# Block loads of a triangular inverse moved from the ScalarE to the SyncE queue, and a quarter of the weights' low parts moved to GpSimd

## The chip, the cores and the metric

The kernel runs on one core of one Trainium2 chip. The metric is the device time of one execution in microseconds, as the median of several runs. The engines are TensorE (PE; its weight loads are shown as PEld), VectorE (DVE), ScalarE (ACT), GpSimd (POOL) and SyncE (SP). DMAs are issued here from the queues of SyncE and ScalarE. An engine carries out its instructions in the order of its queue, so an instruction that waits holds up those behind it on the same engine.

## What is computed

Two layers of a decoder trunk on 256 tokens of width 2048, in float32. Cut to what matters:

```python
for l in range(DEPTH):                       # 2
    hn = rms_norm(h, norm_w[l])
    proj = hn @ w_in[l]                      # 2048 x 8208
    dn_qkv, dn_z, dn_b, dn_a, hg_q, hg_f, hg_i, hg_z = jnp.split(proj, split_points, axis=-1)
    y_a = deltanet_branch(...)               # per chunk: (A + I)^-1 applied, A strictly lower triangular
    y_b = hgrn2_branch(...)
    h = h + jnp.concatenate([y_a, y_b], axis=-1) @ w_out[l]       # 2048 x 2048
    gate = jax.nn.sigmoid(h @ w_ple_gate[l])                      # 2048 x 2048
    h = h + (p[l] @ w_ple_up[l]) * gate                           # 256 x 2048
return rms_norm(h, final_norm_w)
```

Each branch has eight heads of 128, which the kernel handles in four groups of two heads (g = 0 to 3).

## The kernel before

**Weight units.** All weights are packed in the order of use and cut into 392 units (`make_plan`), numbered n. A unit is 128 x 1024 numbers in most cases: two k-tiles of a chunk of 512 columns, or four k-tiles of a narrower chunk (272 or 256 columns). In each layer the input projection has 17 chunks (`in_order`) and 128 units: n = 0 to 127 in the first layer, n = 196 to 323 in the second. Units of chunks 0 and 1 alternate at the start of a layer. Chunk 16, the last, has the last eight units of the stage.

A matmul in full float32 is replaced by three in a faster format: a weight is split into a high part (`whi`, line L400, a copy on ScalarE with rounding) and a low part (`wlo`, L402, raw minus high, on VectorE), and the products are high by high, high by low and low by high. So each unit goes through a DMA from HBM into a raw buffer (`load`, L378, issued by SyncE), the split (`prep`), and 12 matmuls of 512 columns (`products`, L336). Raw, high and low buffers are three each. `ahead(n)` loads up to four units ahead of unit n and splits two units ahead. A load has to wait until the low part of the unit three before it has been made, since both parts are read from the raw buffer. A split waits until TensorE is done with the unit three before.

**Order.** TensorE's instructions keep the order of the program. Beside the units runs the work of the two branches ("mixers"), as generators that yield a number of steps to wait: `tick()` is called once behind each unit, and a generator goes on when its count has run out. The tables `DELAY` and `DELAY_AT` hold the counts, by kind, group and step (`d0q` is DeltaNet, group 0, step q). The other engines' queues are laid out at build time by readiness and program order.

**The inverse.** `Inverse.run` is started when all four DeltaNet groups have delivered their matrices (`given`). It inverts the 16 x 16 diagonal blocks on VectorE (X, L653 and L656), writes them to a scratch in DRAM (`d2`, L658, ScalarE's queue), waits w steps, and reads them back as eight blocks into the tile `Tt` (L662, eight DMAs of 16 KB on ScalarE's queue, all at once). It waits T steps and doubles the block size three times: VectorE transposes (L671), products `pp` and `px` on TensorE, and copies back into `Tt` (L690 with a mask, L712, L740), with waits t16, p16 and so on between them. When it is done, `ready` is set, and each DeltaNet group takes its part (`pz`, in `dv`). In the first layer the waits t16 and p16 are 5 and 1 steps, in the second 2 and 2.

**Work of GpSimd before.** It makes the decay's arguments (`ug`, L769), gate products (`sz`, L590), triangular masks of `QK` (L866), and clears `Tt` (L643).

**Evictions.** Behind each chunk of the input projection, ScalarE copies the sums out of PSUM (`evict`, L597, to a tile named like `hg01fqet`), and the bank is then free for a later chunk.

Of the kernel before, what the change touches and what calls it, by code (L numbers as in the profile page):

```python
# [8 lines left out]
F32 = mybir.dt.float32  # L9
# [3 lines left out]
ALU = mybir.AluOpType  # L13
PSUM = bass.MemoryType.PSUM

DEPTH, D, T, KT = 2, 2048, 256, 16
# [15 lines left out]
def chunk_cols(chunk):  # L32

    return [(START[k], 16) if k == "ba" else (START[k] + 256 * g, 256) for k, g in chunk]
# [2 lines left out]

DELAY = {
    "d": {'c': 1, 'D': 4, 'k': 6, 'q': 7, 'ssq': 1, 'v': 5, 'z0': 1, 'S': 1, 'w': 1, 'z1': 1, 'o': 1, 'y': 3, 'yp': 1},
    "i": {'F': 4, 'F2': 1, 'F3': 1, 'F4': 1, 'w': 2, 'T': 6, 't16': 3, 'p16': 2, 't32': 3, 'p32': 2, 't64': 3, 'p64': 2},  # L40
    "b": {'o': 1, 'g': 4},
    "h": {'c': 1, 'f': 1, 'x2': 1, 'x4': 1, 'x8': 1, 'a': 2, 'x16': 1, 'x32': 1, 'x64': 1, 'u16': 2, 'u64': 1, 'o': 2, 'y': 2, 'yp': 1, 'q': 0},
}

DELAY_AT = {
    "b1g": 5,
    "d0q": 6, "d0y": 2, "d0z1": 2,
    "d2D": 3, "d2k": 4, "d2o": 2, "d2q": 9, "d2y": 2,
    "d3D": 5, "d3ssq": 3,
    "h0o": 4, "h0u16": 1, "h0u64": 3, "h0y": 3, "h0yp": 2,  # L50
    "h1c": 3, "h1o": 1, "h1q": 1, "h1x32": 3, "h1x8": 3, "h1yp": 4,
    "h2c": 2, "h2f": 2, "h2q": 2,
# [10 lines left out]
def in_order():  # L63

    kq = lambda g: (("dk", g), ("dq", g))
    vz = lambda g: (("dv", g), ("dz", g))
    fq = lambda g: (("hf", g), ("hq", g))
    iz = lambda g: (("hi", g), ("hz", g))
    return [(("dz", 0), ("ba", 0)), kq(0), kq(1), kq(2), kq(3), fq(0), iz(0), fq(1), iz(1), fq(2), (("dv", 0),), vz(1),
            iz(2), vz(2), fq(3), vz(3), iz(3)]  # L70
# [96 lines left out]
def trunk(ctx: ExitStack, tc: tile.TileContext, head, xT, x, pT, W, par, fw, cst, msk, eye, out):  # L167
    nc = tc.nc
# [12 lines left out]
    V, S, G = nc.vector, nc.scalar, nc.gpsimd  # L181
# [100 lines left out]
    d2 = dr.tile([256 * 128], F32, name="d2")  # L282
# [20 lines left out]
    def bc1(ap, n):  # L303
        return ap.unsqueeze(1).to_broadcast([ap.shape[0], n, ap.shape[1]])
# [82 lines left out]
    def prep(n):  # L387
        s = steps[n]
        f = s["n"] * len(s["kts"])
        raw = raws.pop(n)  # L390
        if n >= len(steps) - 2:

            ready[n] = [split(raw[:, 512 * j:512 * j + 512], j, None, f"w{n}") for j in range(2)]
            return
        hi = ws.tile([128, 1088], F32R, tag="whi", name=f"whi{n}")
        lo = ws.tile([128, 1088], F32R, tag="wlo", name=f"wlo{n}")
        w = f // 4 if n < 2 else f
        parts = [slice(j, j + w) for j in range(0, f, w)]
        for sl in parts:
            S.activation(hi[:, sl], raw[:, sl], AF.Copy)  # L400
        for sl in parts:
            V.tensor_tensor(lo[:, sl], raw[:, sl], hi[:, sl].bitcast(F32), ALU.subtract)  # L402
        ready[n] = [(hi[:, j * s["n"]:(j + 1) * s["n"]], lo[:, j * s["n"]:(j + 1) * s["n"]]) for j in range(len(s["kts"]))]

    def ahead(n):
        while state["loaded"] < min(len(steps), n + 1 + LOAD) or state["prepped"] < min(len(steps), n + 1 + LOOK):
            if state["loaded"] < min(len(steps), n + 1 + LOAD, state["prepped"] + WRAW):
                load(state["loaded"])
                state["loaded"] += 1
            else:  # L410
                prep(state["prepped"])
                state["prepped"] += 1
# [23 lines left out]
    def run_step(psums, act):  # L436

        n = state["next"]
        s = steps[n]
        ahead(n)  # L440
        if not n:
            for j in range(4):
                for i in (0, 2, 1):
                    for m in range(2):
                        products(n, m, psums, act, js=(j,), parts=(i,))
                if j == 1:
                    warm(1)
        for m in range(2):
            if n:
                products(n, m, psums, act)  # L450
        del ready[n]
        state["next"] = n + 1
        if s["what"] != "up":
            tick()
        return s
# [25 lines left out]
    def split(src, kp, scales, name):  # L481

        hi = ap_.tile([128, 2 * T], F32R, tag="ahi", name=f"{name}hi{kp}")
        lo = ap_.tile([128, 2 * T], F32R, tag="alo", name=f"{name}lo{kp}")
        if scales is None:
            S.activation(hi, src, AF.Copy)
            V.tensor_tensor(lo, src, hi.bitcast(F32), ALU.subtract)
            return hi, lo
        w = 2 * T // len(scales)
        for j, sc in enumerate(scales):  # L490
            S.activation(hi[:, w * j:w * j + w], src[:, w * j:w * j + w], AF.Copy, scale=sc)
        for j, sc in enumerate(scales):
            sl = slice(w * j, w * j + w)
            V.scalar_tensor_tensor(lo[:, sl], src[:, sl], sc, hi[:, sl].bitcast(F32), ALU.mult, ALU.subtract)
        return hi, lo
# [68 lines left out]
    def mix(tag, n, bufs, name):  # L564
        return mp.tile([128, n], F32, tag=tag, name=name, bufs=bufs)

    def v4(ap):
        return ap.rearrange("p (a b) -> p a b", b=128)
# [43 lines left out]
    class Inverse:  # L612


        NT = 4 * NG
# [21 lines left out]
        def run(self):  # L637
            n, Bt, NT = self.n, self.Bt, self.NT


            Tt = self.Tt = v4(mix("Tt", 128 * NT, 1, n + "Tt"))
# [3 lines left out]
            F, X = fx[:, 0], fx[:, 1]  # L645
# [3 lines left out]
            for c in range(1, 16):  # L649
# [3 lines left out]
                i = V.tensor_tensor(pr_[:, :c, :c], X[:, :c, :c], bc1(F[:, :c, c], c), ALU.mult)  # L653
# [5 lines left out]
            yield self.wait("w")  # L659
            for j in range(8):  # L660
                b = slice(16 * j, 16 * j + 16)
                nc.scalar.dma_start(out=Tt[b, :, b], in_=d2.rearrange("(i b a c) -> b a i c", i=NT, b=8, a=16)[j])  # L662
            yield self.wait("T")


# [4 lines left out]
            for b in blocks:  # L670
                i = V.transpose(Tn[b:b + 32], Tt[b:b + 32, :, b:b + 32])  # L671
# [52 lines left out]
            for i in range(NT):  # L724
                for b in (64, 96):
                    c = 64 * (i % 8)
# [7 lines left out]
            for i in range(NT):  # L734
                for b in (0, 32):
                    c = 64 * (i % 8)
# [520 lines left out]
    for l in range(DEPTH):  # L1257
# [25 lines left out]
        for c, k4 in order:  # L1283
# [5 lines left out]
            w = 2 if sum(n for _, n in chunk_cols(ch)) > 272 else 4  # L1289
            for q in range(0, 4, w):  # L1290
# [19 lines left out]
                s = run_step(ps[c], act)  # L1310
# [28 lines left out]
        for c, k4 in order:  # L1339
# [15 lines left out]
            if end and k4[3] == KT - 9:  # L1355

                n = state["next"]
# [46 lines left out]
```

## Time and profile before

| | |
|---|---|
| median of 3 runs | 1256.43 us (1256.11 to 1256.9) |
| profiled execution | 1256.09 us, its span 1254.4 us |
| mean granted TensorE clock | 0.995 |
| PE busy | 1232.5 us (98% of the span) |
| DVE busy | 878.6 us (70%) |
| ACT busy | 779.7 us (62%) |
| POOL busy | 68.5 us (5%) |
| DMA | 218.71 MB, 174 GB/s on average |

Busy time is the time in which an engine had an instruction at work. Matmuls overlap one another, so that a busy PE isn't necessarily at its peak. In rows of the profile, `out<-in` gives the tiles that an instruction writes and reads, `x8` a count, and a bracket the idle time of the engine before the instruction with what ended it. `ACTq` and `SPq` are DMA issues on an engine's queue. Times in the timeline are us from the start of the span, then the duration.

### The profile page before, as it was taken

How to read it: one execution, taken by the hardware profiler on the slowest of the kernel's cores; microseconds unless marked ns; L12 is line 12 of the kernel's file. 1: busy time of each engine (PE TensorE's matmuls, PEld its weight loads, DVE VectorE, ACT ScalarE, POOL GpSimd, SP SyncE). 2: the span in 40 equal slices, each digit the busy share in tenths (PEclk: the TensorE clock that was granted, in tenths of full speed). 3: DMA queues.
4: the chain of work that ended last, by engine and by line, in shares of the span. 5: the costliest groups of instructions: out<-in, count | busy, mean ns of one | idle time of the engine just before them, and what ended most of it. 6: DMA issues, size and time to landing. Idle time of an engine off the chain costs nothing.

```text
span 1254.4 us, 21620 instructions
## 1 busy us (share of the span) xinstructions
PE 1232.5 (98%) x8385; PEld 1034.9 (83%) x8385; DVE 878.6 (70%) x1520; ACT 779.7 (62%) x1397; POOL 68.5 (5%) x64
## 2 busy tenths in 40 slices
PE   9999998999999999999999999989999999999996
PEld 7888887798888888888888888877988888888886
DVE  7777795968668656547667887877776695565566
ACT  7676765676657744447656777566776676444464
POOL 0310000000000100000003100000000000000010
PEclk9999999999999999999999999999999999999998
DMA  8555555545564455555655655645454546555563
GB/s 276 184 178 172 172 173 146 167 134 171 168 218 152 169 178 182 185 192 181 190 182 167 181 159 173 193 120 160 132 164 154 179 145 198 196 183 182 184 202 135
DMA packets 73719, 218.71 MB, mean 174 GB/s; under 512 B 15504, under 2 KB 20752, under 8 KB 73616
## 3 DMA queue, kind: packets, MB, share of 16 engines
q1 hardware_dynamic: 59040, 211.52, 52.6%
q10 hardware_dynamic: 14576, 5.80, 1.7%
q8 instruction: 66, 1.08, 0.3%
q14 instruction: 37, 0.30, 0.1%
HBM read 212.84 MB, written 4.46 MB: 173 GB/s over the span
## 4 chain that ended last, share of the span: by engine, by line
PE 83%; DVE 10%; ACT 2%; issue 2%; DMA 2%; ACTq 0%; SPq 0%; DVEq 0%
PE out L336 14%; PE gate L336 14%; PE in0dk L336 7%; PE in0dv L336 6%; PE in1dk L336 6%; PE in1hf L336 5%; PE in0hf L336 5%; PE in1dv L336 5%; PE in0hi L336 4%; PE in1hi L336 4%; DVE wlo L402 3%; PE up L336 2%; PE in1dz L336 1%; ACT whi L400 1%; PE in0dz L336 1%
## 5 line engine op out<-in xcount | busy, mean ns | idle before, releaser
L402 DVE TENSOR_TENSOR wlo<-raw,whi 128x1024 fp32r<-128x1024 f32 (+1 forms) x392 | 482.1, 1232 | 288.4 <-ACT whi L400 287.6
L400 ACT ACTIVATE whi<-raw 128x1024 fp32r<-128x1024 f32 (+1 forms) x392 | 411.6, 1052 | 333.5 <-PE out L336 89.6
L336 PE MATMUL in1hi<-whi,n1hi 128*128 128x512 f32 x128 | 52.3, 408 | 2.3 <-ACT hg11fqet L597 2.3
L336 PE MATMUL in1hf<-wlo,n1hi 128*128 128x512 f32 x128 | 50.0, 391 | 2.7 <-issue 1.4
L336 PE MATMUL in1dk<-whi,n1hi 128*128 128x512 f32 x128 | 51.2, 400 | 0.0
L336 PE MATMUL in1hf<-whi,n1hi 128*128 128x512 f32 x128 | 51.2, 400 | 0.0
L336 PE MATMUL in1dk<-wlo,n1hi 128*128 128x512 f32 x128 | 50.0, 391 | 0.7 <-DVE wlo L402 0.7
L336 PE MATMUL in1hi<-whi,n1lo 128*128 128x512 f32 x128 | 50.4, 393 | 0.0
L336 PE MATMUL in1hi<-wlo,n1hi 128*128 128x512 f32 x128 | 50.2, 392 | 0.0
L336 PE MATMUL gate<-whi,g0hi 128*128 128x512 f32 x128 | 50.1, 392 | 0.0
L336 PE MATMUL in1dk<-whi,n1lo 128*128 128x512 f32 x128 | 50.0, 391 | 0.0
L336 PE MATMUL in1hf<-whi,n1lo 128*128 128x512 f32 x128 | 49.9, 390 | 0.0
L336 PE MATMUL gate<-whi,g0lo 128*128 128x512 f32 x128 | 49.8, 389 | 0.0
L336 PE MATMUL gate<-wlo,g0hi 128*128 128x512 f32 x128 | 49.8, 389 | 0.0
L336 PE MATMUL in1dv<-whi,n1hi 128*128 128x512 f32 (+1 forms) x128 | 48.2, 377 | 0.0
L336 PE MATMUL in1dv<-whi,n1lo 128*128 128x512 f32 (+1 forms) x128 | 46.6, 364 | 0.0
L336 PE MATMUL in1dv<-wlo,n1hi 128*128 128x512 f32 (+1 forms) x128 | 46.5, 363 | 0.0
L336 PE MATMUL gate<-whi,g1hi 128*128 128x512 f32 (+1 forms) x120 | 45.5, 379 | 0.0
L336 PE MATMUL gate<-wlo,g1hi 128*128 128x512 f32 (+1 forms) x120 | 45.4, 379 | 0.0
L336 PE MATMUL gate<-whi,g1lo 128*128 128x512 f32 (+1 forms) x120 | 45.4, 378 | 0.0
L336 PE MATMUL in0hi<-whi,n0hi 128*128 128x512 f32 x96 | 38.6, 402 | 0.0
L336 PE MATMUL in0hf<-whi,n0hi 128*128 128x512 f32 x96 | 38.4, 400 | 0.0
(1495 smaller groups left out, 3174.8 us busy)
## 6 DMA issues: line engine op xcount, KB each, us to landing
raw<-W SPq DMA_DIRECT2D x384, 512.0 KB, 3.5
raw<-W SPq DMA_DIRECT2D x7, 544.0 KB, 4.2
h<-x SPq DMA_DIRECT2D x4, 512.0 KB, 4.6
xt<-xT SPq DMA_DIRECT2D x3, 512.0 KB, 6.6
out_dram<-h SPq DMA_DIRECT2D x6, 256.0 KB, 2.2
di0d<-di0Bt ACTq DMA_DIRECT2D x4, 256.0 KB, 2.8
di1d<-di1Bt ACTq DMA_DIRECT2D x4, 256.0 KB, 2.3
fw<-fw ACTq DMA_DIRECT2D x2, 512.0 KB, 4.2
```

What stands on the lines that cost most here:

```text
L336: return tc.keep_in_program_order(nc.tensor.matmul(*a, **k))
L400: S.activation(hi[:, sl], raw[:, sl], AF.Copy)
L402: V.tensor_tensor(lo[:, sl], raw[:, sl], hi[:, sl].bitcast(F32), ALU.subtract)
```

## The change

Three things are changed. First, the eight block loads of `Tt` are issued by SyncE instead of ScalarE, with a wait of one step (`b`) behind each, and the wait `T` behind them is 2 steps instead of 6. Second, for every fourth unit of the input projection (n % 4 == 3), from unit 32 on and except in the first and the last chunk, GpSimd subtracts the low part instead of VectorE; nothing else of the unit is changed. Third, four delays of the DeltaNet groups are changed: group 0's `D` is 3 instead of 4 and its `q` 7 (the table's value) instead of 6, group 3's `q` is 5 instead of 7 and its `ssq` 5 instead of 3.

```diff
 DELAY = {
...
-    "i": {'F': 4, 'F2': 1, 'F3': 1, 'F4': 1, 'w': 2, 'T': 6, 't16': 3, 'p16': 2, 't32': 3, 'p32': 2, 't64': 3, 'p64': 2},
+    "i": {'F': 4, 'F2': 1, 'F3': 1, 'F4': 1, 'w': 2, 'b': 1, 'T': 2, 't16': 3, 'p16': 2, 't32': 3, 'p32': 2, 't64': 3, 'p64': 2},
...
 DELAY_AT = {
-    "d0q": 6, "d0y": 2, "d0z1": 2,
+    "d0D": 3, "d0y": 2, "d0z1": 2,
...
-    "d3D": 5, "d3ssq": 3,
+    "d3D": 5, "d3q": 5, "d3ssq": 5,
...
         for sl in parts:
             S.activation(hi[:, sl], raw[:, sl], AF.Copy)
+
+        on = G if s["what"] == "in" and n >= 32 and n % 4 == 3 and s["c"] not in (0, len(in_order()) - 1) else V
         for sl in parts:
-            V.tensor_tensor(lo[:, sl], raw[:, sl], hi[:, sl].bitcast(F32), ALU.subtract)
+            on.tensor_tensor(lo[:, sl], raw[:, sl], hi[:, sl].bitcast(F32), ALU.subtract)
...
             yield self.wait("w")
             for j in range(8):
                 b = slice(16 * j, 16 * j + 16)
-                nc.scalar.dma_start(out=Tt[b, :, b], in_=d2.rearrange("(i b a c) -> b a i c", i=NT, b=8, a=16)[j])
+                nc.sync.dma_start(out=Tt[b, :, b], in_=d2.rearrange("(i b a c) -> b a i c", i=NT, b=8, a=16)[j])
+                yield self.wait("b")
             yield self.wait("T")
```

## The prediction, before the result was known

> **What bounds the kernel now.** I read the page first, then the busy time by stretches, the waits, the chain of waits, and the timeline around the places where TensorE stands still.
>
> ```profile
> PE 1232.5 (98%) x8385; PEld 1034.9 (83%) x8385; DVE 878.6 (70%) x1520; ACT 779.7 (62%) x1397; POOL 68.5 (5%) x64
> L402 DVE TENSOR_TENSOR wlo<-raw,whi 128x1024 fp32r<-128x1024 f32 (+1 forms) x392 | 482.1, 1232 | 288.4 <-ACT whi L400 287.6
> ```
>
> TensorE is busy for 98% of the span, so 21.9 us is all the idle time there is. VectorE is busy for 70%, and more than half of that is one operation, the low part of a weight unit (1.23 us, 392 times). An average hides the stages, so I cut the span into stretches. The columns are span, then busy time and count for PE, PEld, DVE, ACT and POOL, then the granted TensorE clock, DMA share and GB/s.
>
> ```profile
> 146.00:180.00 34.00, 34.00 (x336) 27.91 (x335) 30.57 (x75) 23.95 (x44) 3.38 (x2) 1.00 0.56 177
> 195.00:205.00 10.00, 6.69 (x29) 5.45 (x28) 3.67 (x3) 4.92 (x7) 0.00 (x0) 0.83 0.45 108
> 220.00:250.00 30.00, 29.59 (x613) 23.93 (x612) 28.93 (x61) 19.30 (x30) 1.56 (x1) 1.00 0.53 165
> 300.00:430.00 130.00, 130.00 (x888) 109.34 (x887) 92.07 (x163) 87.97 (x165) 5.27 (x4) 1.00 0.54 179
> 765.00:800.00 35.00, 35.00 (x340) 28.66 (x339) 31.57 (x78) 23.96 (x46) 3.35 (x2) 1.00 0.56 172
> 812.00:822.00 10.00, 7.74 (x33) 6.37 (x33) 3.67 (x3) 4.40 (x6) 0.00 (x0) 0.83 0.56 143
> 830.00:850.00 20.00, 18.68 (x364) 14.81 (x365) 18.47 (x36) 12.80 (x21) 0.00 (x0) 1.00 0.44 134
> 880.00:920.00 40.00, 39.68 (x416) 34.76 (x415) 33.38 (x70) 27.97 (x54) 0.00 (x0) 1.00 0.44 146
> ```
>
> Two stretches of 10 us stand out, one in each layer: TensorE is idle for 3.31 and 2.26 us in them and the granted clock falls to 0.83. Elsewhere (300 to 430) it has no idle time at all. VectorE is nearly full in four stretches: 30.57 of 34, 28.93 of 30, 31.57 of 35, 18.47 of 20. The waits and the timeline name the cause of the two holes:
>
> ```profile
> ACT whi L400 <- DMA di0Tt<-d: 7.3, 1, 7.3
> ACT whi L400 <- DMA di1Tt<-d: 6.2, 1, 6.2
> PE in0hi L336 <- ACT hg01fqet L597: 3.3, 1, 3.3
> PE in1hi L336 <- ACT hg11fqet L597: 2.3, 1, 2.3
> 188.90 0.34 ACTq L658 DMA_DIRECT2D d<-di0fx  x1
> 189.60 1.06 ACT L400 ACTIVATE whi<-raw 128x1024 fp32r<-128x1024 f32 x1
> 190.70 1.22 DVE L402 TENSOR_TENSOR wlo<-raw,whi 128x1024 fp32r<-128x1024 f32 x1 [0.70 <-ACT whi L400]
> 192.63 5.21 ACTq L662 DMA_DIRECT2D di0Tt<-d  x8
> 195.02 0.39 PE L336 MATMUL in0hi<-wlo,n0ahi 128*128 128x512 f32 x1
> 197.95 1.06 ACT L400 ACTIVATE whi<-raw 128x1024 fp32r<-128x1024 f32 x1 [7.28 <-DMA di0Tt<-d]
> 198.91 1.25 ACT L597 ACTIVATE hg01fqet<-in0hf,s0rt 128x512 f32<-128x512 f32 x2
> 811.35 4.05 ACTq L662 DMA_DIRECT2D di1Tt<-d  x8
> ```
>
> ScalarE's queue reaches the eight block loads at 190.66, waits until 192.6 for the scratch write to land, and issues for 5.21 us. The next weight split and the eviction that frees a PSUM bank stand behind it, and TensorE stands behind those.
>
> **The change, part by part.**
>
> *The eight loads leave ScalarE.* ScalarE loses 7.28 and 6.22 us of standing still. With the split and the eviction no longer late, the two TensorE waits go (3.31 + 2.26 us), and so does the slow clock that follows each: 0.17 of 10 us, 1.7 us each. Sum: -(5.0 + 4.0) = -9.0 us. Next late would be the same split waiting for its buffer in the ordinary way, two units ahead of its use: in the rows above the high part ends at 190.66, the low part at 191.92, and the first product that reads it starts at 195.02. At worst the holes stay as they are (0).
>
> *The loads join SyncE.* Behind them on that queue stand the weight loads, and behind those the splits.
>
> ```profile
> SPq L378 <- DVE wlo L402: 815.2, 299, 10.1
> raw<-W SPq DMA_DIRECT2D x384, 512.0 KB, 3.5
> 66.23 2.75 PE in0dk L336 x12
> ```
>
> SyncE waits 2.7 us (815.2/299) before a typical weight load until its raw buffer is free, so it has room for one small issue (5.21/8 = 0.65 us) in each unit of 2.75 us, which is how the new one-step wait spaces them. Only the first can hold the queue, until the scratch write has landed (from 188.90 to 192.63, 3.7 us at most). The low part has 3.1 us to spare at its product (191.92 to 195.02), and a weight load's 3.5 us were already counted in that; so I take 0. If all eight are issued together at a bad place, the queue is held for 3.7 + 4.1 = 7.8 us (4.05 from the second layer's row); less the 3.1 to spare, 4.7 us a layer reach TensorE, or 2.0 if SyncE's ordinary 2.7 of waiting covers its part. Bounds 0 to +9.4, the middle case +4.0 to +9.4.
>
> *The inverse ends later.* Loads one step apart (8) and then 2 instead of 6 steps: 10 steps against 6, so everything after them comes four units, 4 x 2.75 = 11 us, later. Who waits? The chain of waits and the view of one tile tell (the last column but one is the first and last start):
>
> ```profile
> 261.86 1.91 PE di0px L336 x64
> L336 PE MATMUL dn00pz<-dn00R,di0Tt x8: 272/275/275, 295.3 to 310.5; 128*128 128x128 f32 x8
> 228.56 1.85 DVE L690 COPY_PREDICATED di0Tt<-ms,di0px 32x256 f32<-32x256 int32 x4
> 230.44 1.43 DVE L695 STREAM_TRANSPOSE di0T<-di0Tt 32x512 f32<-32x512 f32 x2
> 208.31 2.90 DVE L671 STREAM_TRANSPOSE di0T<-di0Tt 32x512 f32<-32x512 f32 x4
> ```
>
> The last products of the inverse end at 263.8 and its first use is at 295.3: 31 us of cover against 11, so the end costs nothing. Without that cover each step would cost a unit. But its VectorE work moves: 3.3 us (1.85 + 1.43) leaves the full stretch 220 to 250, and 2.9 us moves into it.
>
> *The low parts on GpSimd.* By the plan, 22 units in the first layer and 29 in the second: 51. Their price shows in rows where both engines work:
>
> ```profile
> 233.73 1.56 POOL L590 TENSOR_TENSOR hg01sz<-hg01zs,hg01sz 128x512 f32<-128x512 f32 x1 [55.40 <-ACT hg01sz L471]
> 234.05 2.32 DVE L402 TENSOR_TENSOR wlo<-raw,whi 128x1024 fp32r<-128x1024 f32 x1
> 330.72 1.27 POOL L590 TENSOR_TENSOR hg02sz<-hg02zs,hg02sz 128x512 f32<-128x512 f32 x1 [26.38 <-DVE wlo L402]
> 331.57 1.51 DVE L402 TENSOR_TENSOR wlo<-raw,whi 128x1024 fp32r<-128x1024 f32 x1 [0.90 <-ACT whi L400]
> 233.51 0.50 PE L336 MATMUL in0hf<-wlo,n0hi 128*128 128x512 f32 x1 [0.41 <-DVE wlo L402]
> ```
>
> GpSimd ends at 331.99 and the VectorE subtraction at 333.08, 1.09 us later; in the other pair, 235.29 and 236.37, 1.08 later. So a subtraction of two SBUF operands stands until GpSimd is done: the two take turns, for a whole instruction. GpSimd needs 1.27 us for 512 columns, so at most 2.54 for 1024; I take that, an estimate (the bound below is VectorE's own 1.23). Where VectorE is full, a moved unit takes away 1.23 and blocks 2.54: 1.3 us worse. Where VectorE has idle time, as in 300 to 430 with 38 us of it, nothing follows, and nothing is gained either, since TensorE is full. The moved result itself is in time: 190.66 + 2.54 + one VectorE turn of 1.23 = 194.4, before 195.02. GpSimd's own queue can hold it behind a multiply that waits for ScalarE (the bracket shows 55.4 us before one); that rests on the order of issue, and I count it in the range.
>
> The counts of this operation by stretch (busy, count) let me size it; a quarter of them moves:
>
> ```profile
> 146.00:180.00 34.00, 12.76 (x11) 1.00 0.56 177
> 220.00:250.00 30.00, 10.77 (x8) 1.00 0.53 165
> 765.00:800.00 35.00, 13.28 (x11) 1.00 0.56 172
> 830.00:850.00 20.00, 6.50 (x7) 1.00 0.44 134
> 880.00:920.00 40.00, 13.33 (x11) 1.00 0.44 146
> ```
>
> 146 to 180: 3 x 1.3 = 3.9 against 3.4 idle, +0.5. 765 to 800: the same, +0.5. 220 to 250: 2 x 1.3 - 3.3 + 2.9 = 2.2 against 1.07 idle, +1.1. 830 to 850, with the same inverse work: 2.2 against 1.53, +0.7. 880 to 920: 3.9 against 6.6, 0. Sum +2.8 us. Bounds: nothing hidden, 12 units x 1.3 = +15.6; below, the TensorE waits on a low part go instead, at most 1 us a layer, about -2. I take +2.8 because it is nearest to the stretches' own idle time.
>
> A rule of the Trainium skill speaks against this part. GPSIMD Engine Reference, section 4.1, puts two-input elementwise work on VectorE because GpSimd is about twice as slow, and section 8 says that GpSimd contends with VectorE instructions of two SBUF inputs. The trace agrees: 2.5 against 1.23, and the turns above. By section 3.1's 4497 ns for 2048 columns a unit would hold 2.25 us (an estimate), and the sum would be some 2 us lower.
>
> *The delays.* Group 3's two steps change from 7 + 3 to 5 + 5, the same sum, so the inverse begins where it did; group 0's move by one step each. They lie in 20 to 146 and 640 to 765 where TensorE is full; 0, with +-1 for a coincidence.
>
> **Sum.** -9.0 + 0 + 0 + 2.8 + 0 = -6.2 us, against the profiled execution's own 1256.09 us (its span is 1254.4): 1249.9. That execution lies 0.34 below the median of the runs, so 1250.2.
>
> **Rivals.**
> 1. GpSimd's turns make it slower. Place: the full stretches. If none of the 12 units there finds VectorE idle, +15.6 - 9.0 = +6.6, 1263.0. For it: VectorE stands directly ahead of TensorE at 233.51 with no margin. Against: most stretches have margin, and a TensorE wait gives VectorE time to catch up. It decides for slower from 9 of the 12 units uncovered (9 x 1.3 = 11.7). This is also what the skill's rule amounts to. Chance 0.2.
> 2. The hole moves to SyncE: the middle of +4.0 and +9.4, 6.7, gives 1256.9, no change. For it: the first load still waits for the scratch write, now ahead of weight loads. Against: the loads are issued several units ahead of use. Chance 0.12.
> 3. The turns cost half of the gain and a bit: +4 over my term, 1254.2, at the edge of no change. Chance 0.12.
> 4. VectorE is relieved and nothing is paid: -9.0 - 2 = -11, 1245.4. Chance 0.13.
>
> **How the numbers follow.** My forecast, 1250.2 with its own range of 1247.4 to 1253.8, has 0.43. A measurement of this kernel tells about 0.2% (2.5 us) from no change. Faster: 0.43 + 0.13 and a third of the third rival, 0.6. No change: 0.12 + 0.08, 0.2. Slower: 0.2. The range of 8 in 10 goes from the fourth rival's 1245 to 1260, inside the first.
>
> **What would show it.** Right: no wait of ScalarE for a landing from the scratch, eight loads on SyncE, clock 1.00 in both 10 us stretches, TensorE's waits on evictions gone. The moved low parts take 2.5 us on GpSimd, longer beside VectorE, and VectorE's remaining ones grow well over 1.23 on average. Wrong: new TensorE waits on a low part of over 5 us in all, above all in 146 to 190 and 205 to 250; or splits that wait for weight loads just after the block loads; or GpSimd low parts that start several us after their high part.

## The result, and the profile after

The changed kernel takes 1261.97 us (median of 7 runs, 1259.64 to 1265.19), the kernel before 1256.39 us in the runs beside it. The ratio is 1.0052 with an interval of [1.0037, 1.0066]: half a per cent slower. The forecast was 1250.2 us, with a range of 1245 to 1260. The time is outside it and on the other side, 1 us from the first rival's 1263.0. The profiled execution took 1263.42 us, with a span of 1261.6.

The page of the profile after: busy time of each engine, and the two groups into which the low parts have split.

```profile
PE 1235.8 (98%) x8385; PEld 1035.4 (82%) x8385; DVE 869.8 (69%) x1469; ACT 779.6 (62%) x1397; POOL 199.0 (16%) x115
L404 DVE TENSOR_TENSOR wlo<-raw,whi 128x1024 fp32r<-128x1024 f32 (+1 forms) x341 | 421.3, 1238 | 252.6 <-ACT whi L400 250.9
L404 POOL TENSOR_TENSOR wlo<-raw,whi 128x1024 fp32r<-128x1024 f32 x51 | 133.7, 2621 | 626.1 <-ACT whi L400 599.9
```

All 51 units moved. GpSimd spends 2.62 us on one, VectorE 1.24 on one that it kept. VectorE's busy time went down by 8.8 us (878.6 to 869.8), and the kernel became slower. Busy time doesn't say where.

TensorE's idle time is now 1261.6 - 1235.8 = 25.8 us against 21.9 before, and its busy time is 3.3 us longer. The stretches (columns as in the prediction: span, busy time and count of PE, PEld, DVE, ACT and POOL, granted clock, DMA share, GB/s):

```profile
146.00:180.00 34.00, 31.86 (x318) 25.51 (x318) 29.60 (x65) 23.75 (x45) 9.28 (x4) 1.00 0.48 157
180.00:195.00 15.00, 13.36 (x72) 10.55 (x67) 12.90 (x27) 5.87 (x11) 3.62 (x3) 1.00 0.44 140
195.00:205.00 10.00, 10.00 (x52) 8.49 (x51) 3.68 (x3) 5.61 (x7) 1.40 (x1) 1.00 0.75 219
300.00:430.00 130.00, 128.50 (x871) 107.60 (x869) 85.46 (x153) 87.69 (x164) 24.37 (x12) 0.99 0.51 175
812.00:822.00 10.00, 8.99 (x41) 7.21 (x40) 6.74 (x13) 5.87 (x10) 2.39 (x1) 1.00 0.60 165
```

The hole at 195 to 205 is gone: TensorE is busy for 10.00 of 10 at clock 1.00, where it had 6.69 at 0.83. The second layer's stretch is back at clock 1.00 too, with 1.01 us idle for 2.26. But 146 to 180, which had no idle time before, now has 2.14 us, 180 to 195 has 1.64, and 300 to 430 has 1.50. TensorE's largest waits (the view of waits: total, times, longest):

```profile
PE dn00pz L336 <- DVE dn00R L891: 2.2, 1, 2.2
PE in1hf L336 <- DVE wlo L404: 1.9, 3, 1.0
PE in0hf L336 <- DVE wlo L404: 1.8, 3, 1.0
PE dn02yp L339 <- DVE dn02yt L577: 1.5, 1, 1.5
PE dn12yp L339 <- DVE dn12yt L577: 1.5, 1, 1.5
PE in0hf L336 <- ACT hg00zs L589: 1.2, 1, 1.2
```

The two waits on the evictions `hg01fqet` and `hg11fqet` (3.3 and 2.3) are no longer there, and ScalarE waits for no landing from the scratch. New waits have come, and the largest are on VectorE, several of them not on low parts: `dn00R` and `dn02yt` are steps of the DeltaNet group. A smaller one is on another eviction, the copy `hg00zs` (1.2 us, and as much in the second layer); ahead of it ScalarE stood 4.32 us for VectorE's `hg00X`, until 172.07. The timeline shows what makes those late (start, duration, engine and line; the bracket is the idle time before it):

```profile
164.49 4.93 POOL L404 TENSOR_TENSOR wlo<-raw,whi 128x1024 fp32r<-128x1024 f32 x1 [11.87 <-ACT whi L400]
167.26 3.24 DVE L404 TENSOR_TENSOR wlo<-raw,whi 128x1024 fp32r<-128x1024 f32 x1
178.18 0.20 DVE L655 TENSOR_TENSOR di0pr<-di0fx 128x25 f32<-128x25 f32 x1
178.69 2.69 POOL L404 TENSOR_TENSOR wlo<-raw,whi 128x1024 fp32r<-128x1024 f32 x1 [9.27 <-ACT whi L400]
179.05 2.40 DVE L655 TENSOR_TENSOR di0pr<-di0fx 128x36 f32<-128x36 f32 x1
275.95 4.18 POOL L404 TENSOR_TENSOR wlo<-raw,whi 128x1024 fp32r<-128x1024 f32 x1 [15.54 <-ACT whi L400]
277.79 3.28 DVE L577 SCALAR_TENSOR_TENSOR hg01yt<-hg01o,hg01f,hg01sz 128x128 f32<-128x128 f32 x4
291.92 2.39 POOL L404 TENSOR_TENSOR wlo<-raw,whi 128x1024 fp32r<-128x1024 f32 x1 [11.79 <-ACT whi L400]
292.18 2.41 DVE L1014 TENSOR_TENSOR hg02X<-hg02G 128x256 f32<-128x256 f32 x1
294.85 0.41 DVE L1014 TENSOR_TENSOR hg02X<-hg02G 128x256 f32<-128x256 f32 x1
297.92 0.67 DVE L891 TENSOR_TENSOR dn00R<-dn00pv,invn 128x512 f32<-128x512 f32 x1
400.85 2.55 POOL L404 TENSOR_TENSOR wlo<-raw,whi 128x1024 fp32r<-128x1024 f32 x1 [13.75 <-ACT whi L400]
401.45 2.22 DVE L1021 TENSOR_TENSOR hg03X<-hg03X,hg03k 128x256 f32<-128x256 f32 x1 [0.32 <-ACT hg03X L1019]
404.00 1.13 DVE L577 SCALAR_TENSOR_TENSOR dn02yt<-dn02o,fo,dn02sz 128x128 f32<-128x128 f32 x4
```

At 292.18 a VectorE subtraction that takes 0.41 us in the next row takes 2.41: it lies beside a GpSimd low part from its start until just after that one's end. All that is queued behind it on VectorE moves by 2.0 us. It is the second such stop on the way to `dn00R`: at 277.79 four rows `hg01yt` take 3.28 us, where they take 1.14 in the form with no low part on GpSimd (form 3 below), 2.1 more. In that form `dn00R` ends 1.6 us before the weight load of its product begins (289.36 and 291.0), which would have covered most of one stop. The two together make TensorE stand for 2.2 us.

The same lies at 179.05 (36 columns in 2.40 us, where 25 took 0.20 at 178.18) and at 401.45, ahead of `dn02yt`. The blocking goes the other way too: the low part begun at 164.49 lasts 4.93 us, beside VectorE instructions that follow one another closely, and at 167.26 it is VectorE's own low part that takes 3.24.

### The profile page after: what moved, and what is told of

The parts are those of the page before. It is cut to its first block, busy times and chain, and to the rows that moved or that the text cites. A ratio compares the mean times of both kernels' runs of the same rounds, so it can differ in the third digit from the quotient of the medians.

```text
span 1261.6 us, 21643 instructions
## 1 busy us (share of the span) xinstructions
PE 1235.8 (98%) x8385; PEld 1035.4 (82%) x8385; DVE 869.8 (69%) x1469; ACT 779.6 (62%) x1397; POOL 199.0 (16%) x115
## 3 DMA queue, kind: packets, MB, share of 16 engines
q8 instruction: 66, 1.08, 0.4%
## 4 chain that ended last, share of the span: by engine, by line
PE 83%; DVE 11%; ACT 3%; issue 2%; DMA 1%; SPq 0%; ACTq 0%; DVEq 0%
PE out L336 14%; PE gate L336 13%; PE in1dk L336 7%; PE in0dk L336 7%; PE in0hf L336 6%; PE in1hf L336 6%; PE in1dv L336 5%; PE in1hi L336 4%; PE in0hi L336 4%; PE in0dv L336 3%; DVE wlo L404 3%; PE up L336 2%; ACT whi L400 1%; PE in1dz L336 1%; PE in0dz L336 1%
## 5 line engine op out<-in xcount | busy, mean ns | idle before, releaser
L404 DVE TENSOR_TENSOR wlo<-raw,whi 128x1024 fp32r<-128x1024 f32 (+1 forms) x341 | 421.3, 1238 | 252.6 <-ACT whi L400 250.9
L404 POOL TENSOR_TENSOR wlo<-raw,whi 128x1024 fp32r<-128x1024 f32 x51 | 133.7, 2621 | 626.1 <-ACT whi L400 599.9
L336 PE MATMUL in0hf<-wlo,n0hi 128*128 128x512 f32 x96 | 37.6, 392 | 1.6 <-DVE wlo L404 1.6
```

What stands on the lines that cost most here:

```text
L336: return tc.keep_in_program_order(nc.tensor.matmul(*a, **k))
L404: on.tensor_tensor(lo[:, sl], raw[:, sl], hi[:, sl].bitcast(F32), ALU.subtract)
```

## The experiments

In the expectations theory A is that GpSimd's turns hold up VectorE and make the loss; the others put it down to what their text says. Each time is a median, and its ratio is to the kernel before on the same chip.

**1. The block loads alone.** Before, with the loads on SyncE one step apart, and nothing else.

```
-    nc.scalar.dma_start(out=Tt[b, :, b], ...)
+    nc.sync.dma_start(out=Tt[b, :, b], ...)
+    yield self.wait("b")                # and 'b': 1, 'T': 2
```

> The kernel before with the eight block loads on SyncE one step apart and T of 2 steps; low parts on VectorE, delays as before. Theory A (GpSimd's turns with VectorE cost the time, the queue change gains): faster by 8 to 13 us, 1243 to 1248, no clock dip around 200 and 815. Theory B (the inverse that comes four units later costs the time): slower by 3 to 8 us. Theory C (the four delays cost it): as A.

Measured: 1246.94 us, ratio 0.9935 [0.9922, 0.9949], 8.2 us faster.

**2. The low parts alone.** Before, with `on = G` for the 51 units.

```
-    V.tensor_tensor(lo[:, sl], raw[:, sl], hi[:, sl].bitcast(F32), ALU.subtract)
+    on.tensor_tensor(lo[:, sl], raw[:, sl], hi[:, sl].bitcast(F32), ALU.subtract)
```

> The kernel before with 51 low parts on GpSimd and nothing else changed. Theory A: slower by 10 to 20 us, 1266 to 1276, less where the hole behind the block loads gives VectorE time to catch up. Theory B: within 2 us of before. Theory C: within 2 us of before.

Measured: 1283.62 us, ratio 1.0226 [1.0211, 1.0241], 28.4 us slower, well above what the theory of the turns gave. The sign is as expected, the size isn't. In this form TensorE waits for moved low parts themselves as well: 2.0 us in each layer ahead of an `hf` product and 1.0 us at two others, 5.0 us in all, where after has no such wait.

**3. All but the low parts.** After, with `on = V`.

```
-    on = G if s["what"] == "in" and n >= 32 and n % 4 == 3 and ... else V
+    on = V
```

> The changed kernel with all low parts back on VectorE. Theory A: faster than before by 8 to 13 us, 1243 to 1248, and so 13 to 20 us faster than the changed kernel. Theory B: slower than before by 3 to 8 us. Theory C: slower than before by 3 to 8 us, and slower than the queue change alone by as much.

Measured: 1246.35 us, ratio 0.9929 [0.9917, 0.9942]. So within the whole change the low parts cost 1261.97 - 1246.35 = 15.6 us.

**4. The delays alone.** Before, with the four changed delays.

```
-    "d0q": 6, "d0y": 2, "d0z1": 2,
+    "d0D": 3, "d0y": 2, "d0z1": 2,
-    "d3D": 5, "d3ssq": 3,
+    "d3D": 5, "d3q": 5, "d3ssq": 5,
```

> The kernel before with the four DeltaNet delays alone changed. Theories A and B: within 2 us of before. Theory C: slower by 4 to 8 us.

Measured: 1254.34 us, ratio 0.9995 [0.9986, 1.0004]: no change.

These four leave one sign for each part: the loads gain, the delays alone do nothing, and the low parts lose more than the loads gain.

**5. What of the loads' gain is the hole?** Before, with all eight loads on SyncE at once and the six steps kept, so that the rest of the inverse stays where it was.

```
-    nc.scalar.dma_start(out=Tt[b, :, b], ...)
+    nc.sync.dma_start(out=Tt[b, :, b], ...)
```

> The kernel before with only the queue of the eight block loads changed to SyncE: all eight at once, T of 6 steps, no wait between them. If taking them off ScalarE is all of the gain (theory A): 1245 to 1249, as the one-by-one form (1246.9). Rival (the gain comes from the inverse's VectorE work being four units later, out of the full stretches): only the two holes go, some 9 us, and the waits on a low part stay, 1248 to 1252. Rival (SyncE is held by eight loads in a row): splits that wait for weight loads, 1250 or more.

Measured: 1249.87 us, ratio 0.9950 [0.9938, 0.9963], 5.8 us faster: just above the first theory's 1245 to 1249 and inside the range of the rival that puts the rest down to the later inverse. That rival's sign, waits on a low part that stay, is not there: they come to 3.3 us in before, 1.2 here and 1.3 in form 1. The waits on evictions are gone here too, but new ones stand in their place. TensorE's two largest waits in this form:

```profile
PE hg00yp L339 <- DVE hg00yt L575: 1.8, 1, 1.8
PE hg10yp L339 <- DVE hg10yt L575: 1.3, 1, 1.3
```

Its timeline ahead of the first of them:

```profile
191.94 4.65 SPq L662 DMA_DIRECT2D di0Tt<-d  x8
196.69 1.34 SPq L378 DMA_DIRECT2D raw<-W  x3
200.87 1.06 ACT L400 ACTIVATE whi<-raw 128x1024 fp32r<-128x1024 f32 x1 [1.47 <-DMA raw<-W]
203.95 0.28 ACT L609 ACTIVATE hg00f<-hsso,epsc 128x4 f32<-128x4 f32 x1
205.22 1.13 DVE L575 SCALAR_TENSOR_TENSOR hg00yt<-hg00o,hg00f,hg00sz 128x128 f32<-128x128 f32 x4
```

The eight loads hold SyncE for 4.65 us. The weight load behind them is late, ScalarE's split waits 1.47 us for it at 200.87, `hg00f` stands behind that split and a second one (203.00) on ScalarE, `hg00yt` behind `hg00f`, and TensorE behind `hg00yt`. That is the second rival, in a small size: 1.8 + 1.3 = 3.1 us of standing still, and the granted clock is 0.57 from 207 to 211, 0.43 x 4 = 1.7 us more. The holes themselves are then worth some 5.8 + 3.1 + 1.7 = 10.6 us, an estimate that adds the three from one profiled execution.

The late load alone doesn't explain the wait: in form 1 a split waits even longer for its load, 2.53 us at 198.78, but only that one stands ahead of `hg00f`, which starts at 202.09. Form 1's stretch from 195 to 205, with the loads one by one, has no such wait of TensorE, and 812 to 822 shows the same busy times:

```profile
195.00:205.00 10.00, 10.00 (x57) 8.61 (x56) 4.72 (x7) 6.72 (x16) 0.00 (x0) 1.00 0.70 218
```

The two forms differ in the steps behind the loads as well, so how much of the 2.4 us between them is SyncE's queue and how much the later inverse was not separated; the intervals of the two overlap.

**6. Loads and low parts, old delays.** After, with the delays of before.

```
-    "d0D": 3, "d0y": 2, "d0z1": 2,
+    "d0q": 6, "d0y": 2, "d0z1": 2,
-    "d3D": 5, "d3q": 5, "d3ssq": 5,
+    "d3D": 5, "d3ssq": 3,
```

> The changed kernel with the four delays as before: one-by-one loads on SyncE and 51 low parts on GpSimd. The low parts alone cost 28 us on the kernel before and 15.6 us on the kernel with new loads and delays. If the moved inverse is what softens the cost: 1260 to 1265, as the changed kernel. If the four delays are what softens it: 1270 to 1276.

Measured: 1270.76 us, ratio 1.0119 [1.0106, 1.0133]. The same 51 low parts cost 28.4 us on the kernel before, 1270.76 - 1246.94 = 23.8 with the loads moved, and 15.6 with loads and delays. The delays, worth nothing alone, take 23.8 - 15.6 = 8.2 us off the price of the low parts (8.8 off the time). So the price isn't a property of the operation. It depends on what VectorE has queued when the turn comes.

**7. Shorter turns.** After, with each moved low part in two instructions of 512 columns.

```
-    for sl in parts:
+    for sl in parts if on is V else [slice(0, f // 2), slice(f // 2, f)]:
```

> The changed kernel, but each moved low part is made by two GpSimd instructions of 512 columns instead of one of 1024, so that each blocks VectorE half as long. Theory A (VectorE stands while GpSimd holds the shared access, for a whole instruction): 1252 to 1258, VectorE's longest instructions shorter by some 1.2 us. Rival D (the price is that the low part itself, or the raw buffer, is late): 1262 to 1265, since the second half ends no sooner.

Measured: 1262.06 us, ratio 1.0050 [1.0036, 1.0064], the same as after: theory A's gain did not come, and the time is the one that rival D gave. But D's cause hardly shows. TensorE waits for no GpSimd low part in after, and here for 0.4 us in each layer at a weight load. As to the raw buffer, splits wait for loads 19.8 us in all in after against 10.2 in form 3, but 17.3 in form 1, which has no loss. Its timeline at the places shown above:

```profile
164.46 6.06 POOL L404 TENSOR_TENSOR wlo<-raw,whi 128x512 fp32r<-128x512 f32 x2 [11.41 <-ACT whi L400]
178.81 1.32 DVE L655 TENSOR_TENSOR di0pr<-di0fx 128x36 f32<-128x36 f32 x1
```

A blocked instruction is blocked half as long (1.32 where it was 2.40), but two instructions are now blocked (the next one takes 1.53), and the pair that begins at 164.46 ends 6.06 us later where the single one took 4.93. This fits a price that goes with the time that GpSimd holds in all, not with the length of one turn.

**8. The same operation elsewhere.** After, with no low part of the input projection on GpSimd and every second one of the output and gate products (60 units on the page; the expectation counts 62).

```
-    on = G if s["what"] == "in" and n >= 32 and n % 4 == 3 and ... else V
+    on = G if s["what"] in ("out", "gate") and n % 2 == 1 and n < 384 else V
```

> The changed kernel with no low part of the input projection on GpSimd, but every second one of the output projection and the gate instead (62 units), where VectorE is busy for some 58% and has little to do beside low parts. Theory A (the price is paid where VectorE is full or its result is awaited): within 2 us of 1246.4, the time without GpSimd. Rival D (a low part on GpSimd is late wherever it is, or its raw buffer): slower than 1246.4 by 10 us or more, with waits of TensorE on GpSimd's low parts.

Measured: 1249.62 us, ratio 0.9950 [0.9937, 0.9962]; 3.3 us above form 3, or 0.05 us for a unit against 15.6/51 = 0.31 in the input projection. By the ratios it is 0.9950 - 0.9929 = 0.21% or 2.6 us, and the two intervals overlap a little, so that even this small price is barely clear of noise. It lies between the two expectations. The page's group of the moved low parts:

```profile
L404 POOL TENSOR_TENSOR wlo<-raw,whi 128x1024 fp32r<-128x1024 f32 x60 | 146.0, 2434 | 232.1 <-ACT whi L400 228.3
```

TensorE's largest wait on one of them:

```profile
PE gate L336 <- POOL wlo L404: 1.4, 3, 0.6
```

More units, the same 2.4 us each, a fifth of the price at most.

**9 and 10. Which units cost.** The start of each weight unit on TensorE, set beside that of form 3, shows at which units after falls behind: 4.3 us over units 47 to 59, 2.5 around 83 and 87, 3.5 at 115 and 119, 4.6 over 243 to 255, 3.5 at 311 and 315. Form 3 in its turn loses 3.2 us near unit 268 that after doesn't. Together 18.4 - 3.2 = 15.2 us, of the 15.9 between the two profiled spans (1261.6 and 1245.7). Form 9 leaves these 14 units to VectorE and moves the other 37; form 10 moves the 14 alone.

```
+    ... and n not in (47, 51, 55, 59, 83, 87, 115, 119, 243, 247, 251, 255, 311, 315) else V     # form 9
+    on = G if n in (47, 51, 55, 59, 83, 87, 115, 119, 243, 247, 251, 255, 311, 315) else V       # form 10
```

> The kernel after with 37 of the 51 low parts on GpSimd; the 14 units 47 to 59, 83, 87, 115, 119, 243 to 255, 311 and 315 have theirs on VectorE. These are the units about which TensorE's start times in the kernel after fall behind those of the form with no low part on GpSimd (1246.35): by 4.3, 2.5, 3.5, 4.6 and 3.5 us there, and hardly at the other units. Theory A (the price is paid at the places where VectorE's next awaited result stands behind a GpSimd turn; elsewhere it is nothing): 1246 to 1250. Rival (each moved low part costs about the same, 15.6/51 = 0.31 us, and the places are only where the lag shows): 1246.35 + 37 x 0.31 = 1257.8.

> The kernel after with only these 14 low parts on GpSimd (units 47 to 59, 83, 87, 115, 119, 243 to 255, 311, 315), all others on VectorE. Theory A: nearly the whole price of the 51, 1246.35 + 12 to 18 = 1258 to 1264. Rival (even price): 1246.35 + 14 x 0.31 = 1250.7.

Measured: form 9 takes 1245.6 us, ratio 0.9924 [0.991, 0.9938]; form 10 takes 1263.7 us, ratio 1.0071 [1.0057, 1.0084]. The 37 units cost nothing and the 14 cost all of it; an even price for each unit (1257.8 and 1250.7) is refuted. By the ratios to form 3's, 1.0071 - 0.9929 = 1.42% or 17.8 us, which is 1.3 us for each of the 14 on average (the 15.6 of all 51 differs from it by no more than the intervals allow). The average hides unlike places: in after, the starts jump by 2.5 us at unit 87 and by 3.5 each at 119 and 315, 1.7 of each 3.5 through a fall of the clock, and not at all at 83, 115 and 311. Unit 83 still counts, as the first of the two stops ahead of `dn00R`; 115 and 311 were not tried apart. Form 10's group of moved low parts on the page:

```profile
L404 POOL TENSOR_TENSOR wlo<-raw,whi 128x1024 fp32r<-128x1024 f32 x14 | 43.1, 3077 | 190.7 <-ACT whi L400 190.7
```

TensorE's largest waits in form 10 are those of after, in the second layer too (`in1hf` 2.0, `dn12yp` 1.4):

```profile
PE dn00pz L336 <- DVE dn00R L891: 2.2, 1, 2.2
PE in0hf L336 <- DVE wlo L404: 2.0, 3, 1.0
PE dn02yp L339 <- DVE dn02yt L577: 1.4, 1, 1.4
```

Of smaller ones, those on `hg00zs` and `hg10zs` are gone, and two of 0.7 us on a GpSimd low part are new. Form 9 has no wait on `dn00R` or a `yt`, and its waits on VectorE's low parts are 0.4 us at most. Its group on the page:

```profile
L404 POOL TENSOR_TENSOR wlo<-raw,whi 128x1024 fp32r<-128x1024 f32 x37 | 92.5, 2499 | 508.5 <-ACT whi L400 487.7
```

In form 9's stretches TensorE is full, or nearly so, where after stood:

```profile
146.00:180.00 34.00, 33.65 (x333) 27.38 (x332) 30.11 (x71) 24.86 (x45) 1.91 (x2) 1.00 0.57 180
180.00:195.00 15.00, 15.00 (x70) 12.48 (x69) 12.47 (x26) 7.82 (x12) 0.00 (x0) 1.00 0.47 155
300.00:430.00 130.00, 130.00 (x885) 109.24 (x884) 85.35 (x155) 87.57 (x164) 19.28 (x10) 1.00 0.54 174
```

From 300 to 430 VectorE is as busy as in after (85.35 and 85.46), GpSimd does 10 pieces of work instead of 12, and TensorE's idle time goes from 1.50 us to none. Forms 9, 3 and 1 are the fastest measured, and their intervals overlap: the low parts are best left alone, or moved where they do nothing.

One rival was not tried apart. The queues are laid out at build time, so that moving low parts also changes the order of VectorE's other instructions. At `dn00R` it adds little: beside the start of its unit, `dn00R` ends 4.2 us later in after than in form 3, and the two stops make 2.1 + 2.0 = 4.1 of that. For the other places this was not worked out.

## Why the prediction was wrong, point by point

**The loads leave ScalarE, -9.0: right.** The loads alone gave -8.2, and in the two stretches the waits and the clock came out as described. That the two numbers are so close is partly luck: form 1 has a wait of its own, 1.8 us ahead of `hg01pa`, with the clock at 0.72 from 231 to 237 (1.7 us), and has lost others of the second layer (1.4 and 1.3 us in before, 0.9 in form 1).

**SyncE, 0 (bounds 0 to +9.4): right in time, not in every sign.** A split that waits for a weight load behind block loads, which the prediction named as a sign against it, is there in after, without reaching TensorE, which is busy for 10.00 of 10 from 195 to 205:

```profile
195.52 0.83 SPq L664 DMA_DIRECT2D di0Tt<-d  x2
196.45 0.39 SPq L378 DMA_DIRECT2D raw<-W  x1
201.61 1.06 ACT L400 ACTIVATE whi<-raw 128x1024 fp32r<-128x1024 f32 x1 [1.17 <-DMA raw<-W]
```

The two splits before it, at 195.22 and 198.04, wait for loads too (1.08 and 1.76 us), but these were issued from 191.47 on, ahead of the block loads. All eight at once cost about 4.8 with the clock's share, within the middle case's +4.0 to +9.4, though not by its sum of 4.7 or 2.0 for each layer: 3.5 came in the first and 1.3 in the second.

**The inverse later, 0: right on the end, short on the move.** The view of one tile, of after (durations, first and last start):

```profile
L336 PE MATMUL di0px<-di0Tt,di0P x256: 177/191/240, 241.9 to 282.5; 32*32 32x16 f32 x64, 32*32 32x32 f32 x32, 64*32 64x64 f32 x32
L336 PE MATMUL dn00pz<-dn00R,di0Tt x8: 275/275/377, 298.7 to 314.0; 128*128 128x128 f32 x8
```

The last products end near 283, some 19 us later than before and not 11: they stand behind unit 82, where before has them behind unit 77. That is five units and not four (form 1, with the loads alone, has four), and a unit there isn't worth 2.75 us: from the start of unit 77 to that of 82 before takes 20.4 us (258.8 to 279.2), 4.1 each, since other products lie between. TensorE itself is 3.3 us ahead of before at unit 80. Their use is still 16 us away, and waits for `dn00R`, not for the inverse.

**The delays, 0: right alone, wrong together.** The step held for the kernel before (-0.8, no change) but not beside the moved low parts, where it was worth -8.8. Which of the four does it, and by which of VectorE's instructions, was not separated.

**The low parts, +2.8: the step that failed.** Measured +15.6, and +23.8 or +28.4 without the delays. The step had the cost of a turn right and its cover wrong. Four points in it:

- The mechanism was read rightly from two rows of before: a subtraction on VectorE stands until GpSimd's instruction is done. So was the size: 2.54 us was estimated for a turn and the median is 2.40 (the mean, with GpSimd's own waiting, 2.62). The 1.3 us of loss for an uncovered unit is the average of the 14, but not what one place shows: there a whole turn, less the margin, reaches TensorE, and the fall of the clock comes on top.
- The count was wrong. The step set the loss of each stretch against its VectorE idle time, so that 12 units x 1.3 shrank to 2.8. Idle time of a stretch is no cover: from 146 to 180 VectorE has 4.40 of 34 us idle in after, and TensorE still stands for 2.14. What matters is whether the instruction that TensorE needs next is behind the turn.
- The places were wrong for the same reason. "Where VectorE has idle time, as in 300 to 430 with 38 us of it, nothing follows" is refuted by `dn02yt` at 404.00. In before it starts at 397.97, with its product right behind it:

```profile
397.97 1.13 DVE L575 SCALAR_TENSOR_TENSOR dn02yt<-dn02o,fo,dn02sz 128x128 f32<-128x128 f32 x4
399.38 0.60 PE L339 MATMUL dn02yp<-cs,dn02yt 128*128 128x128 f32 x4
```

  The four `yt` end at 399.10 and their product starts 0.28 us later: in the trace of before that was the sign to look for. Of the five places of loss, 146 to 195 and its counterpart in the second layer touch stretches on the prediction's list; those of `dn00R` and of the two `yt` do not. From 220 to 250 and 830 to 850, where the step put 1.8 of its 2.8, the unit starts show 0.5 us in the first layer and nothing in the second.
- It counted blocked low parts alone. Other VectorE instructions with two SBUF operands are blocked too, and they are short: one of some 0.2 us stood for 2.40. (That the moved result itself is in time held in after, but not in form 2, where 5.0 us were lost on it.)

The low parts' bound, +15.6, was worked out as 12 x 1.3 and equals the measured +15.6. That is partly chance: 14 units at 1.3 give 17.8 alone. The first rival, GpSimd's turns with no cover in the full stretches, named the mechanism and came within 1 us. The 1 us is luck in part: its place was the full stretches, and 2.5 + 3.5 + 3.5 = 9.5 of the 18.4 us of jumps lie outside them. Its "against" (margin, and time to catch up) is what did not hold at the five places, and did hold at the other 37 units.

The Trainium skill's GPSIMD Engine Reference, section 8, says that GpSimd contends with VectorE instructions of two SBUF inputs; the 2.40 us at 179.05 agree. The same page of the Trainium skill, section 4.1, puts two-input elementwise work on VectorE. Forms 8 to 10 agree: none beats form 3 by more than the measurement tells.

## What to carry to other kernels

Before work moves to GpSimd, look in the timeline for each VectorE result that TensorE takes within a microsecond of its end, and ask what a stop of one whole GpSimd instruction ahead of it would do, or two; the busy share of a stretch can't answer that. This is read off the places of one kernel and was not tried on another. Where one part of a change gains and another loses, take each alone and then all but each: here the parts gave -8.2, 0 and +28.4 alone, and the price of the last fell to 15.6 in company. Compare the start of each unit of the bounding engine between two traces: five jumps told which 14 of 51 units to leave, and two runs then showed that these make the price.

## What was not expected of the hardware

GpSimd waits too: a low part took up to 4.93 us beside closely following VectorE instructions, and in form 10 the 14 of them average 3.08 us (6.10 at most), against 2.50 for form 9's 37.

The granted clock doesn't fall after every short wait. After TensorE's wait of 1.5 us for `dn02yt` the clock in the profile of after is 0.69 and 0.74 over two stretches of 3 us:

```profile
405.00:408.00 3.00, 3.00 (x132) 2.62 (x133) 3.00 (x6) 0.00 (x0) 0.00 (x0) 0.69 0.47 172
408.00:411.00 3.00, 3.00 (x11) 2.37 (x10) 2.81 (x12) 1.74 (x4) 0.00 (x0) 0.74 0.83 295
```

In form 10's stretches it stays at 1.00 after such a wait of 1.4 us, and falls behind the wait for `dn00R` instead:

```profile
405.00:408.00 3.00, 2.32 (x133) 1.90 (x133) 3.00 (x8) 0.33 (x1) 0.00 (x0) 1.00 0.49 175
300.00:303.00 3.00, 3.00 (x11) 2.33 (x10) 2.22 (x4) 2.02 (x4) 0.00 (x0) 0.65 0.57 180
```

So 0.31 x 3 + 0.26 x 3 = 1.7 us come with a wait or stay away; over 406.1 to 409.6 alone the clock of after is 0.51. The two traces are of two kernels, but executions of one kernel differ as well: the seven of after have mean granted clocks from 0.994 (1264.15 us) to 0.998 (1259.64 us). The Trainium skill's TensorE: Matmul & The Clock Gate, Part 1, puts the fall of the clock behind an idle window of about 3.4 us; here it fell behind 1.5 us, so the measurement decides.
